# One-tile input loads, and work that changes engine, in a one-core hybrid mLSTM and DeltaNet block

## The chip, the cores and the metric

The kernel runs on one core of one Trainium2 chip. The metric is device time in microseconds (us); lower is better. A core has a matrix engine (TensorE, PE in the profile), an elementwise engine (VectorE, DVE), an activation engine (ScalarE, ACT), a general engine (GpSimd, POOL) and a synchronising engine (SyncE, SP) that here only issues transfers. Each engine runs its instructions in the order in which they stand in its own queue. Transfers are issued from SyncE, ScalarE or GpSimd and stand in the issuing engine's order until they are issued.

## The reference

One decoder layer over 512 tokens of width 2048, in float32:

```python
u = _rmsnorm(h, norm_w)
proj = jnp.matmul(u, w_in)                    # 24624 output columns
# mLSTM branch: 8 heads, q and k of 128, v of 256, exponential input gate, running-max stabiliser
# DeltaNet branch: 16 heads of 128; causal conv of width 4 and SiLU on q, k, v;
#   q and k divided by their L2 norms; chunks of 64:
lhs = strict_lower(beta * (k @ k.T) * decay) + eye
w_val, w_k = solve(lhs, [v * beta, k * beta * exp(gam)])
# recurrence over chunks: u = w_val - w_k S ; o = q_dec S + (qk*decay) u ; S = g S + k_end^T u
y_a = h_a @ w_out[:2048];  y_b = h_b @ w_out[2048:]
out = rmsnorm(h + sigmoid(gate_a) * y_a + sigmoid(gate_b) * y_b) * final_norm_w
```

## The kernel before

**Arithmetic.** Each float32 operand of a large product is split into two parts, hi and lo (`split_hi` is a cast on ScalarE, line 144; `split_lo` a subtraction on VectorE, line 147), and TensorE runs three products: hi with uh, hi with ul, lo with uh (lines 258 to 260 in `proj_cm`, 583 to 585 in the seven-product stage, 1423 to 1425 in the output stage).

**Stages.** First x is loaded, turned on TensorE (`make_u`, line 313), weighted by the norm weights and split into uh and ul, while the first block of input-projection columns is being multiplied (`proj_cm` with `before=first_block`). The token factor 1/rms comes later, from `square_x`. Then come the remaining first projections and a long stage of products (`seven_stage`) to about 1130 us, eight DeltaNet units of two heads each (`dn_unit`), in whose products the mLSTM heads are interleaved, and the output projection with the final norm.

**Order of the work.** TensorE's order is the order of the code. On the other engines a planner sorts by its own simulated times and priorities; `urgent` raises the priority, and `behind("A")` puts an instruction after the newest cast on ScalarE ("V": the newest lo split). Transfers on SyncE are sorted by the same planner.

**Steps.** Six large products make one call of `tick()`, called a step below. Everything of the mixers is written as generators started with `start(gen, wait)`; `yield n` means n steps later. A DeltaNet unit has 48 steps: 16 each for k, v and q.

**The start (lines 264 to 346).** x is held in four tiles, one for each 128 tokens. `load_x(a, b)` issues one transfer for each of them, alternately from SyncE and ScalarE, in five calls with column ranges that widen; weight tiles (`load_raw`, SyncE, 256 KB) stand between the first ones. `load_norms` loads the norm weights on GpSimd's queue and turns them on TensorE (line 109) before x. `make_u(kt)` turns one 128-column slice with four transposes; uh is written by ScalarE (line 314), ul by VectorE (line 315). Slices 0 to 3 stand ahead of the first product: two from the loop over `UA`, two from `before`.

**A DeltaNet unit.** After k's projection `conv_silu` and `silu_end` make k, and `turn` with `travel` make a token-major copy `ke`: a transpose in 32 x 32 blocks on VectorE, four transfers to DRAM and one back, all on SyncE. `dn_front_k` forms k k^T times the decay into `aq` and reads the key norms off its diagonal (line 926, VectorE), from which come `nk` and `cs` = beta over the squared norm. `aq` is scaled by cs (lines 941 to 944, ScalarE), its diagonal 32 x 32 blocks go through DRAM into `ls`, and 31 substitution passes on VectorE (lines 970 and 972, two to a step) invert them into `xi`; `xi` goes through DRAM into `tt`, and VectorE transposes that into `tn` (line 988). Counting steps from the end of k's projection, cs stands at 10, the scaling at 13 and 14, the first pass at 24, the transfers of xi at 39 and tn at 55. `dn_back` joins the blocks into the inverse of 128 x 128 in products p1 to p4, with evictions between them (s1, tb, ta, s3). For the second head of a unit the norm factor has not been multiplied in yet on one block; the eviction of p3 (line 1057) does it on 64 partitions on VectorE while ScalarE negates the other 64 (line 1056). The products of line 1063 read the first half. `dn_back` also multiplies v by the norms `nk` (line 1035). `dn_chain` then runs the recurrence.

Of the kernel before, what the change touches and what calls it, by code (L numbers as in the profile page):

```python
# [58 lines left out]
def hybrid_body(  # L59
# [119 lines left out]
    def split_next():  # L179
        raw, nk, n = raws[len(parts)]  # L180
        with tc.high_priority(offset=2 * PRIO if len(parts) > SAHEAD else 0):
            hi = wp.tile([P, nk, n], F32R, tag="wh", name="wh", bufs=NSPL)
            lo = wp.tile([P, nk, n], F32R, tag="wl", name="wl", bufs=NSPL)
            with ExitStack() as first:
                if len(parts) == 1:
                    first.enter_context(tc.issue_after(done["V"]))
                    first.enter_context(tc.issue_after(done["A"]))
                split_hi(hi, raw)
                split_lo(lo, raw, hi)
        parts.append((hi, lo))  # L190
# [56 lines left out]
    def proj_cm(col0, before=None):  # L247
        ps = [psj.tile([P, S], F32, tag="pj", name="pj") for _ in range(2)]
        for kt0 in range(0, KT, KP):
            hi, lo = next_w("i", col0, kt0)  # L250
            if before is not None:
                for k in range(KP):
                    before(kt0 + k)
            for j in range(2):
                for k in range(KP):
                    kt = kt0 + k
                    wsl = slice(j * P, (j + 1) * P)
                    T.matmul(ps[j], hi[:, k, wsl], uh[:, kt, :], start=(kt == 0), stop=False)  # L258
                    T.matmul(ps[j], hi[:, k, wsl], ul[:, kt, :], start=False, stop=False)  # L259
                    T.matmul(ps[j], lo[:, k, wsl], uh[:, kt, :], start=False, stop=(kt == KT - 1))  # L260
                tick()
        return ps
# [4 lines left out]
    load_norms(p0, psw)  # L267
    xts = [p0.tile([P, D], F32, tag=f"x{c}", name=f"xt{c}") for c in range(NC)]

    def load_x(a, b):  # L270
        for c in range(NC):
            (nc.scalar if c % 2 else nc.sync).dma_start(xts[c][:, a:b], x[c * P:(c + 1) * P, a:b])

    load_x(0, NB)
    load_raw()
    load_x(NB, 2 * NB)
    load_raw()
    for a in range(2 * NB, D, NO):
        load_x(a, a + NO)
    wg = p0.tile([P, KT, 48], F32, tag="wg", name="wg")  # L280
# [12 lines left out]
    def square_x(c, i):  # L293
        xt, at = xts[c][:, i * HD:(i + 1) * HD], ss[:, c, i:i + 1]
        jk = p0.tile([P, HD], F32, tag="jk", name="jk", bufs=2)
        with tc.issue_after(done["V" if i else "A"]):
            if i:
                V.scalar_tensor_tensor(out=jk, in0=xt, scalar=1.0, in1=xt, op0=ALU.mult, op1=ALU.mult, accum_out=at)
            else:
                A.activation(jk, xt, AF.Square, accum_out=at)  # L300
# [8 lines left out]
    def make_u(kt):  # L309
        pool, tg = ((psw, "wk"), (pso, "o"))[kt % 2]  # L310
        pt = pool.tile([P, S], F32, tag=tg, name="put")
        for c in range(NC):
            T.transpose(pt[:, c * P:(c + 1) * P], xts[c][:, kt * P:(kt + 1) * P], ident)
        done["A"] = A.activation(uh[:, kt, :], pt, AF.Copy, scale=normc[:, kt:kt + 1]).ins
        done["V"] = V.scalar_tensor_tensor(out=ul[:, kt, :], in0=pt, scalar=normc[:, kt:kt + 1],
                                           in1=uh[:, kt, :].bitcast(F32), op0=ALU.mult, op1=ALU.subtract).ins

    UA = 2
    for kt in range(UA):
        make_u(kt)  # L320
# [548 lines left out]
    def travel(o, dst, out, apart):  # L869
# [13 lines left out]
        yield 4  # L883
# [4 lines left out]
    def dn_front_k(hs, kq, u):  # L888
# [26 lines left out]
        for j in range(2):  # L915
# [6 lines left out]
            with urgent():  # L922
                V.tensor_tensor(out=aq[:, :, 0, :], in0=pk, in1=u["dm"][j][0], op=ALU.mult)
                jk = wkb.tile([P, P], F32, tag="jd", name="jd", bufs=1)
                for c in range(NC):
                    V.scalar_tensor_tensor(out=jk, in0=aq[:, c, 0, :], scalar=1.0, in1=ident, op0=ALU.mult,
                                           op1=ALU.mult, accum_out=nk[:, j, c:c + 1])
            yield 1
        V.tensor_scalar(out=nk, in0=nk, scalar1=EPS, scalar2=None, op0=ALU.add)
# [5 lines left out]
        yield 3  # L935
# [29 lines left out]
        for i in range(BS - 1):  # L965
# [7 lines left out]
            if i % 2:  # L973
                yield 1
# [11 lines left out]
        yield 16  # L986
# [25 lines left out]
    def dn_back(hs, kq, u):  # L1012
# [19 lines left out]
        for j in range(2):  # L1032
            vn = u["vs"][j]
            with behind("V"):
                V.tensor_tensor(out=vn, in0=vn, in1=bc(u["nk"][:, j, :], P), op=ALU.mult)
# [7 lines left out]
        with urgent(2):  # L1043
            V.tensor_copy(ta[32:64, :, 0:32], p2[32:64, 1])
        for q in range(2):
# [9 lines left out]
        with urgent():  # L1055
            A.mul(s3[64:128], p3[64:128], -1.0)
            V.tensor_tensor(out=s3[0:64], in0=p3[0:64], in1=u["cs"][0:64, 1, :].unsqueeze(2).to_broadcast([64, NC, 64]),
                            op=ALU.mult)
# [5 lines left out]
        with urgent():  # L1064
            V.tensor_copy(tb[0:64, 0:NC, 64:128], p4[0:64])
            A.mul(tb[0:64, NC:2 * NC, 64:128], p4[64:128], -1.0)
# [68 lines left out]
    def dn_unit(p):  # L1135
# [7 lines left out]
        for j in range(2):  # L1143
# [3 lines left out]
            start(silu_end(kq[j][:, 0, :], (kq[j][:, 0, :], ke)), 4 + 3 * j, front)  # L1147
# [653 lines left out]
```

## Time and profile before

| what | us |
|---|---|
| median of three runs | 2156.34 |
| lowest and highest | 2155.92, 2158.04 |
| the profiled execution's own time | 2156.07 |
| its span, first to last instruction | 2154.3 |
| TensorE busy | 2119.7 (98%) |
| VectorE busy | 1735.1 (81%) |
| ScalarE busy | 1043.4 (48%) |
| GpSimd busy | 453.5 (21%) |

All views are of one profiled execution on the chip; times start at its first instruction. The page gives busy time for each engine. The view of waits gives, for an engine, the time it sat idle before an instruction and what ended that. The time line lists instructions in order, with start, duration, engine, line, tile names and shapes, and in brackets the idle time before them. In the view of one line three numbers are the shortest, the median and the longest duration in nanoseconds. A view of stretches gives the busy time of each engine between two moments. In names, `put` is turned x, `pj` a projection in PSUM, `wr`, `wh` and `wl` a weight tile as loaded and its two parts.

### The profile page before, as it was taken

How to read it: one execution, taken by the hardware profiler on the slowest of the kernel's cores; microseconds unless marked ns; L12 is line 12 of the kernel's file. 1: busy time of each engine (PE TensorE's matmuls, PEld its weight loads, DVE VectorE, ACT ScalarE, POOL GpSimd, SP SyncE). 2: the span in 40 equal slices, each digit the busy share in tenths (PEclk: the TensorE clock that was granted, in tenths of full speed). 3: DMA queues.
4: the chain of work that ended last, by engine and by line, in shares of the span. 5: the costliest groups of instructions: out<-in, count | busy, mean ns of one | idle time of the engine just before them, and what ended most of it. 6: DMA issues, size and time to landing. Idle time of an engine off the chain costs nothing.

```text
span 2154.3 us, 32062 instructions
## 1 busy us (share of the span) xinstructions
PE 2119.7 (98%) x10545; PEld 1754.5 (81%) x10545; DVE 1735.1 (81%) x3035; ACT 1043.4 (48%) x2022; POOL 453.5 (21%) x690
## 2 busy tenths in 40 slices
PE   8999999999999999999999999999999999999998
PEld 6888888888888888888888888888888878787786
DVE  4888788788888777777858898988888888569887
ACT  4444455445544554454445536546455454345345
POOL 0000000000004000000013434326243263243211
PEclk9999999999999999999999999999999999999999
DMA  5456666667667766776766677668687677678895
GB/s 170 147 171 208 209 202 206 202 216 226 210 220 244 244 211 209 233 232 195 250 213 175 169 183 187 174 168 201 178 206 174 161 185 207 192 227 281 243 298 226
DMA packets 448961, 444.48 MB, mean 206 GB/s; under 512 B 197333, under 2 KB 305082, under 8 KB 448666
## 3 DMA queue, kind: packets, MB, share of 16 engines
q1 hardware_dynamic: 377882, 335.12, 53.5%
q0 software_dynamic: 24864, 73.17, 10.8%
q10 hardware_dynamic: 46048, 34.16, 4.9%
q8 instruction: 82, 1.34, 0.3%
q14 instruction: 85, 0.70, 0.1%
HBM read 348.92 MB, written 97.59 MB: 207 GB/s over the span
## 4 chain that ended last, share of the span: by engine, by line
PE 69%; issue 12%; DVE 8%; DMA 5%; ACT 3%; POOL 1%; SPq 1%; ACTq 0%; DVEq 0%; POOLq 0%
PE ps L584 14%; PE ps L585 14%; PE ps L583 14%; PE pj L258 6%; PE pj L260 6%; PE pj L259 6%; DVE wl L147 2%; PE py L1423 1%; PE py L1424 1%; PE py L1425 1%; ACT wh L144 1%; DVE kq L843 1%; DVE xi L972 1%; DVE tmp L970 1%; ACT njk L860 1%
## 5 line engine op out<-in xcount | busy, mean ns | idle before, releaser
L144 ACT CAST wh<-wr 128x512 fp32r<-128x512 f32 (+1 forms) x522 | 374.2, 717 | 416.4 <-PE pj L259 201.9
L147 DVE TENSOR_TENSOR wl<-wr,wh 128x512 fp32r<-128x512 f32 (+1 forms) x522 | 436.6, 837 | 162.1 <-ACT wh L144 158.2
L258 PE MATMUL pj<-uh,wh 128*128 128x512 f32 x896 | 375.9, 420 | 4.4 <-ACT wh L144 3.9
L260 PE MATMUL pj<-uh,wl 128*128 128x512 f32 x896 | 351.9, 393 | 0.0
L259 PE MATMUL pj<-ul,wh 128*128 128x512 f32 x896 | 350.0, 391 | 0.0
L584 PE MATMUL ps<-wl,uh 128*128 128x512 f32 x752 | 292.7, 389 | 1.1 <-DVE wl L147 1.1
L583 PE MATMUL ps<-wh,uh 128*128 128x512 f32 x752 | 292.6, 389 | 0.8 <-DVE X L637 0.8
L585 PE MATMUL ps<-wh,ul 128*128 128x512 f32 x752 | 292.6, 389 | 0.0
L144 ACT CAST wh<-t 128x1024 fp32r<-128x1024 f32 x120 | 126.4, 1053 | 290.8 <-PE ps L585 186.2
L538 POOL DMA_DIRECT2D t_d<-ts x104 | 56.7, 545 | 922.2 <-DVE ts L525 844.6
L584 PE MATMUL ps<-wl,suh 128*128 128x512 f32 x624 | 242.9, 389 | 0.5 <-DVE wl L147 0.5
L583 PE MATMUL ps<-wh,suh 128*128 128x512 f32 x624 | 242.8, 389 | 0.0
L585 PE MATMUL ps<-wh,sul 128*128 128x512 f32 x624 | 242.7, 389 | 0.0
L144 ACT CAST wh<-ts 128x512 fp32r<-128x512 f32 x240 | 148.1, 617 | 187.3 <-DVE ts L543 158.8
L147 DVE TENSOR_TENSOR wl<-t,wh 128x1024 fp32r<-128x1024 f32 x120 | 146.8, 1223 | 82.3 <-ACT wh L144 81.9
L260 PEld LDWEIGHTS pj<-uh,wl 128*128 128x128 f32 x896 | 168.4, 188 | 37.6 <-DVE wl L147 0.5
L258 PEld LDWEIGHTS pj<-uh,wh 128*128 128x128 f32 x896 | 169.2, 189 | 35.7 <-ACT wh L144 4.3
L259 PEld LDWEIGHTS pj<-ul,wh 128*128 128x128 f32 x896 | 169.5, 189 | 28.5
L147 DVE TENSOR_TENSOR wl<-ts,wh 128x512 fp32r<-128x512 f32 x240 | 164.3, 685 | 32.7 <-ACT wh L144 31.2
L584 PEld LDWEIGHTS ps<-wl,uh 128*128 128x128 f32 x752 | 141.2, 188 | 30.7 <-DVE wl L147 1.5
L583 PEld LDWEIGHTS ps<-wh,uh 128*128 128x128 f32 x752 | 141.2, 188 | 30.6 <-DVE X L637 1.2
L585 PEld LDWEIGHTS ps<-wh,ul 128*128 128x128 f32 x752 | 141.2, 188 | 29.2
(355 smaller groups left out, 3833.8 us busy)
## 6 DMA issues: line engine op xcount, KB each, us to landing
wr<-in_w_in_dram SPq DMA_DIRECT2D x744, 256.0 KB, 3.6
wr<-in_w_out_dram SPq DMA_DIRECT2D x138, 256.0 KB, 4.9
t_d<-ts POOLq DMA_DIRECT2D x104, 256.0 KB, 3.6
wr<-t_d SPq DMA_DIRECT2D x104, 256.0 KB, 3.8
tg_d<-X ACTq DMA_DIRECT2D x16, 256.0 KB, 4.3
tg_d<-to ACTq DMA_DIRECT2D x16, 256.0 KB, 4.1
v<-v_d SPq DMA_DIRECT2D x8, 512.0 KB, 6.1
mg<-g_d SPq DMA_DIRECT2D x16, 256.0 KB, 3.6
```

The source lines that it names most:

```text
L144: newest["A"] = A.copy(hi, src).ins
L147: newest["V"] = V.tensor_tensor(out=lo, in0=src, in1=hi.bitcast(F32), op=ALU.subtract).ins
L258: T.matmul(ps[j], hi[:, k, wsl], uh[:, kt, :], start=(kt == 0), stop=False)
L259: T.matmul(ps[j], hi[:, k, wsl], ul[:, kt, :], start=False, stop=False)
L260: T.matmul(ps[j], lo[:, k, wsl], uh[:, kt, :], start=False, stop=(kt == KT - 1))
L538: queue.dma_start(t2_d[b % 2, i], ts[:, 0, :])
L583: T.matmul(ps[t], ah, hi, start=(g == "A" and i == 0), stop=False, skip_group_check=True)
L584: T.matmul(ps[t], ah, lo, start=False, stop=False, skip_group_check=True)
L585: T.matmul(ps[t], al, hi, start=False, stop=(i == KH - 1), skip_group_check=True)
L843: V.scalar_tensor_tensor(out=dst, in0=yp[:, j:j + S], scalar=convc[:, 48 * j + ct:48 * j + ct + 1], in1=dst, op0=ALU.mult, op1=ALU.add)
L860: A.activation(jk, pk[:, c, :], AF.Square, accum_out=dst[:, c:c + 1])
L970: V.tensor_tensor(out=tv, in0=ls[:, i, i + 1:BS].unsqueeze(1).to_broadcast([P, m, n]), in1=xi[:, 0:m, i].unsqueeze(2).to_broadcast([P, m, ...
```

## The change

In the start, x becomes one tile of all four token blocks, and each range of columns (a slab) is one transfer on SyncE. A weight tile is loaded between all slabs, so that five are ahead instead of two. A Square of two ones is put first on ScalarE. The first slab is issued ahead of the norm weights. The first weight tile is split right behind slice 0's uh and ul, and slices 2 and 3 are turned between the two column halves of the first products, instead of before both.

In a unit, the key norms are taken by ScalarE from the turned copy `ke` (sum of squares, `token_norms`) instead of by VectorE from the diagonal. The v factors go to ScalarE in eight multiplications. The eviction of p3 becomes one negation of all 128 partitions on ScalarE; the factor cs is multiplied into `ta` on GpSimd before, and p4's second half is then copied without a sign. Several waits are set anew: the read back of a turned tile comes a step sooner, k's second copy starts a step sooner, cs comes at step 15, the scaling at 17 and 18, the first pass at 28, and the wait behind the passes is 12 instead of 16. In the last unit alone four passes go to a step.

```diff
@@ split_next
-                if len(parts) == 1:
+                if len(parts) < 2:
                     first.enter_context(tc.issue_after(done["V"]))
                     first.enter_context(tc.issue_after(done["A"]))
@@ proj_cm
-            if before is not None:
-                for k in range(KP):
-                    before(kt0 + k)
             for j in range(2):
+                if before is not None and j == (kt0 == 0):
+                    for k in range(KP):
+                        before(kt0 + k)
                 for k in range(KP):
@@ the start
+    xt = p0.tile([P, NC, D], F32, tag="x", name="xt")
+    warm = p0.tile([P, 2], F32, tag="warm", name="warm")
+    A.activation(warm, ones2, AF.Square)
+
+    def load_x(a, b):
+        nc.sync.dma_start(xt[:, :, a:b], x[:, a:b].rearrange("(c p) d -> p c d", p=P))
+
+    load_x(0, NB)
     load_norms(p0, psw)
-    xts = [p0.tile([P, D], F32, tag=f"x{c}", name=f"xt{c}") for c in range(NC)]
-
-    def load_x(a, b):
-        for c in range(NC):
-            (nc.scalar if c % 2 else nc.sync).dma_start(xts[c][:, a:b], x[c * P:(c + 1) * P, a:b])
-
-    load_x(0, NB)
     load_raw()
     load_x(NB, 2 * NB)
     load_raw()
     for a in range(2 * NB, D, NO):
         load_x(a, a + NO)
+        load_raw()
...
     UA = 2
-    for kt in range(UA):
-        make_u(kt)
+    make_u(0)
+    split_next()
+    make_u(1)
@@ travel
-        yield 4
+        yield 3
         with urgent(2):
             nc.sync.dma_start(dst, d.rearrange("(n j) r a c -> (j r) n (a c)", n=NC))
@@ dn_front_k
                 V.tensor_tensor(out=aq[:, :, 0, :], in0=pk, in1=u["dm"][j][0], op=ALU.mult)
-                jk = wkb.tile([P, P], F32, tag="jd", name="jd", bufs=1)
-                for c in range(NC):
-                    V.scalar_tensor_tensor(out=jk, in0=aq[:, c, 0, :], scalar=1.0, in1=ident, op0=ALU.mult,
-                                           op1=ALU.mult, accum_out=nk[:, j, c:c + 1])
             yield 1
+        yield 2
+        for j in range(2):
+            with behind("A"):
+                token_norms(u["ke"][j], nk[:, j, :])
+            yield 2 - j
...
-        yield 3
+        yield 2
         for j in range(2):
             aq = u["aq"][j]
...
-            if i % 2:
+            if i % 4 == 3 or (i % 2 and hs[0] < 2 * UNITS[-1]):
                 yield 1
...
-        yield 16
+        yield 12
         with urgent(), behind("V"):
             V.transpose(tn.rearrange("p g m -> p (g m)"), tt.rearrange("p g t -> p (g t)"))
@@ dn_back
-            with behind("V"):
-                V.tensor_tensor(out=vn, in0=vn, in1=bc(u["nk"][:, j, :], P), op=ALU.mult)
+            with behind("A"):
+                for c in range(NC):
+                    A.mul(vn[:, c, :], vn[:, c, :], u["nk"][:, j, c:c + 1])
...
             V.tensor_copy(ta[32:64, :, 0:32], p2[32:64, 1])
+        G.tensor_tensor(out=ta[:, NC:], in0=ta[:, NC:], in1=u["cs"][0:64, 1, :].unsqueeze(2).to_broadcast([64, NC, 64]),
+                        op=ALU.mult)
...
         with urgent():
-            A.mul(s3[64:128], p3[64:128], -1.0)
-            V.tensor_tensor(out=s3[0:64], in0=p3[0:64], in1=u["cs"][0:64, 1, :].unsqueeze(2).to_broadcast([64, NC, 64]),
-                            op=ALU.mult)
+            A.mul(s3, p3, -1.0)
...
             V.tensor_copy(tb[0:64, 0:NC, 64:128], p4[0:64])
-            A.mul(tb[0:64, NC:2 * NC, 64:128], p4[64:128], -1.0)
+            A.copy(tb[0:64, NC:2 * NC, 64:128], p4[64:128])
@@ dn_unit
-            start(silu_end(kq[j][:, 0, :], (kq[j][:, 0, :], ke)), 4 + 3 * j, front)
+            start(silu_end(kq[j][:, 0, :], (kq[j][:, 0, :], ke)), 4 + 2 * j, front)
```

`square_x` and `make_u` read the one tile instead of four.

More of the change, by code (lines that the diff above doesn't have):

```diff
@@ L293, in square_x @@
     def square_x(c, i):
-        xt, at = xts[c][:, i * HD:(i + 1) * HD], ss[:, c, i:i + 1]
+        at = ss[:, c, i:i + 1]
+        xc = xt[:, c, i * HD:(i + 1) * HD]
         jk = p0.tile([P, HD], F32, tag="jk", name="jk", bufs=2)
@@ L297, in square_x @@
             if i:
-                V.scalar_tensor_tensor(out=jk, in0=xt, scalar=1.0, in1=xt, op0=ALU.mult, op1=ALU.mult, accum_out=at)
+                V.scalar_tensor_tensor(out=jk, in0=xc, scalar=1.0, in1=xc, op0=ALU.mult, op1=ALU.mult, accum_out=at)
             else:
-                A.activation(jk, xt, AF.Square, accum_out=at)
+                A.activation(jk, xc, AF.Square, accum_out=at)
     def token_factors():
@@ L312, in make_u @@
         for c in range(NC):
-            T.transpose(pt[:, c * P:(c + 1) * P], xts[c][:, kt * P:(kt + 1) * P], ident)
+            T.transpose(pt[:, c * P:(c + 1) * P], xt[:, c, kt * P:(kt + 1) * P], ident)
         done["A"] = A.activation(uh[:, kt, :], pt, AF.Copy, scale=normc[:, kt:kt + 1]).ins
```

## The prediction

> **What bounds the kernel now.** I read the stretches first, to see where TensorE is not busy (columns: stretch, length, then busy time of PE, PEld, DVE, ACT and POOL, the granted clock, the DMA share, GB/s):
>
> ```profile
> 0.00:54.00 54.00, 43.94 (x212) 34.63 (x213) 25.96 (x49) 24.59 (x42) 3.49 (x14) 1.00 0.58 171
> 54.00:1140.00 1086.00, 1085.53 (x4807) 898.55 (x4806) 875.62 (x1163) 514.70 (x739) 88.09 (x161) 1.00 0.66 212
> 1140.00:1835.00 695.00, 686.76 (x4077) 572.21 (x4076) 591.33 (x1459) 362.84 (x1003) 279.38 (x396) 1.00 0.73 182
> ```
>
> TensorE bounds it. The opening leaves 10.1 us idle, the next 1086 us only 0.5, the DeltaNet units (1140 to 1835) 8.2. So the change can take time out only at the start and in the units, and what it takes out at the start reaches the end unless a later wait gives it back. From 1100 us on, TensorE's longest waits are these (total, times, longest):
>
> ```profile
> PE p L1063 <- DVE s L1057: 5.3, 4, 1.7
> PE py L1424 <- DVE wl L147: 2.8, 1, 2.8
> PE pw L1093 <- DVE r L1088: 1.5, 2, 0.8
> ```
>
> **The start.** The time line of ScalarE, then that of TensorE:
>
> ```profile
> 0.74 9.86 ACTq L272 DMA_DIRECT2D xt<-in_x_dram  x10
> 10.69 1.28 ACT L314 ACT_TABLE_LOAD   x1 [10.69 <-DMA xt<-in_x_dram]
> 11.99 1.26 ACT L314 ACTIVATE uh<-put,normc 128x512 fp32r<-128x512 f32 x2
> 13.14 0.62 ACT L144 CAST wh<-wr 128x512 fp32r<-128x512 f32 x1
> ```
>
> ```profile
> 4.97 0.25 PE L109 MATMUL pprm<-ident,nrow 16*128 16x16 f32 x1 [4.97 <-DMA nrow<-in_norm_w_dram]
> 5.16 2.39 PE L313 MATMUL put<-ident,xt 128*128 128x128 f32 x10
> 8.38 1.54 PE L313 MATMUL put<-ident,xt 128*128 128x128 f32 x6 [0.84 <-DMA xt<-in_x_dram]
> 13.81 0.79 PE L258 MATMUL pj<-uh,wh 128*128 128x512 f32 x1 [3.88 <-ACT wh L144]
> ...
> 16.64 0.60 PE L258 MATMUL pj<-uh,wh 128*128 128x512 f32 x1
> 17.07 0.42 PE L259 MATMUL pj<-ul,wh 128*128 128x512 f32 x1
> 17.33 0.39 PE L260 MATMUL pj<-uh,wl 128*128 128x512 f32 x1
> 17.56 0.39 PE L258 MATMUL pj<-uh,wh 128*128 128x512 f32 x1
> ...
> 18.26 0.93 PE L313 MATMUL put<-ident,xt 128*128 128x128 f32 x7
> ```
>
> ScalarE issues ten x transfers until 10.60, then loads its table, then makes uh and the first weight cast; only then, at 13.81, can the first product run, though sixteen transposes were ready at 9.92. The change takes the x transfers off ScalarE and has the table loaded by a two-column Square at the beginning, beside the wait for x.
>
> The new order is worked out from these rows. The transposes still begin at 5.16: the first TensorE instruction waits for the norm weights, which nothing moves, and x's first 256 columns had landed by then although they shared the queues. Four transposes at 0.24 (2.39/10) end at 6.1, one uh (1.26/2 = 0.63) at 6.75, the cast (0.62) at 7.4. Six products at the early spacing of 0.43 (16.64 to 17.07) then run to 10.0. The next eight transposes, now behind them, take 1.06 (0.93/7 each) to 1.9; the other six products take 1.4 (17.33 to 17.56 is 0.23) to 2.6. The following transposes so begin at 12.4 to 14.5 in place of 18.26: a gain of 3.8 to 5.9. I take 13.1, **-5.2 us**, with the clock rising in the middle.
>
> The spacing falls from 0.43 to 0.23 some 3.3 us after the first product, though transposes had run from 5.16 to 9.92. The Trainium skill, "TensorE: Matmul & The Clock Gate", section "Part 4: PE-mode transpose", says that transposes do not count as activity that releases the clock, which speaks against putting eight of them between the first products; the trace fits it, but its 3.9 us pause would explain the same. By that rule the slow end of my bounds, -3.8, would hold.
>
> What has to follow does so with cover. One SyncE queue now carries five slabs of x (4 MB) with the weight tiles between them. Queued behind are the fifth weight tile, which must wait for the first split to free its buffer (due about 8.4, before the queue gets there), the gate weights and the small parameters. The slabs for the next products are the second and third of five, and those were already the order of the old queues. If the cover were gone, a slab or the gate weights would be late by up to 2 us: that is inside the bounds.
>
> **The units.** Rows of the line view (min/median/max ns):
>
> ```profile
> L926 DVE SCALAR_TENSOR_TENSOR jd<-aq,ident x64: 248/292/1032, 1146.5 to 1756.7; 128x128 f32<-128x128 f32 x64
> L926 DVE DVE_READ_ACCUMULATOR jd<-aq,ident x64: 74/81/84, 1146.7 to 1756.9; 128x1 f32 x64
> L860 ACT ACTIVATE njk<-qn x64: 292/310/313, 1211.3 to 1833.7; 128x128 f32<-128x128 f32 x64
> L860 ACT ACTIVATION_READ_ACCUMULATOR njk<-qn x64: 185/187/190, 1211.5 to 1833.9; 128x1 f32 x64
> L1035 DVE TENSOR_TENSOR vt<-vt,nk x16: 678/684/882, 1224.7 to 1849.1; 128x512 f32<-128x512 f32 x16
> L944 ACT ACTIVATE aq<-aq,cs x32: 384/387/402, 1152.3 to 1758.9; 128x128 f32<-128x128 f32 x32
> ```
>
> Each of the eight units takes from VectorE 8 x (0.292 + 0.081) = 3.0 us of key norms, 2 x 0.684 = 1.4 of value factors and one 0.4 eviction: 4.8. It gives ScalarE 8 x (0.310 + 0.187) = 4.0 and 8 x 0.387 = 3.1: 7.1. The eviction's sign half was on ScalarE already; it now takes all 128 partitions at the same free length. Where that eviction stands (ScalarE's half, VectorE's half, and the stretch around, in the fourth unit):
>
> ```profile
> 1498.16 0.38 ACT L1056 ACTIVATE s<-p 64x256 f32<-64x256 f32 x1
> 1500.94 0.41 DVE L1057 TENSOR_TENSOR s<-p,cs 64x256 f32<-64x256 f32 x1
> 1486.00:1498.00 12.00, 12.00 (x144) 9.74 (x144) 8.62 (x29) 8.31 (x25) 8.12 (x12) 1.00 0.94 246
> ```
>
> ScalarE's half is 2.8 us ahead of VectorE's, which is the one that TensorE waits for, 1.3 us on average in four units. Moved whole to ScalarE, the 5.3 us of waits go, unless ScalarE becomes later by more than 2.8 - 1.3 = 1.5 us. It was busy 8.3 of those 12 us; 7.1 come and the 3.2 of the key scaling (4 x 0.387 and eight shorter ones) move four steps later, so 12.2 of 12: just full. I take **-4.5**, between -5.3 and 0. The multiplication by cs goes to GpSimd, with two waits of three steps (eleven microseconds at the step worked out below) before TensorE reads it; the stretch above has GpSimd busy 8.1 of 12 us, so it is covered: 0, and the wait itself, up to 1.5 a unit, if the queue there is that late. Less work on VectorE should end some of the 1.5 us at L1088: **-0.5** (0 to -1.5). A crowded ScalarE may hold the split of the weights or a state copy: **+0.5** (0 to +5).
>
> The key norms now come from the turned tile, so they wait on ScalarE for its round trip through DRAM, with the next weight casts behind them, and VectorE and TensorE behind those. The turned tile is written two steps after its SiLU, at 6 and 8, and its norms stand at 12 and 14: six steps, 10.9 us, against a trip of about 8.7 (both below). So 2 us are spare. The steps that the code counts go from 10 to 15 for cs and from 24 to 28 for the first step of the inverse, and the wait behind the inverse is cut from 16 to 12, so that its transpose tn stays at step 55. Its cover shrinks by four steps. Rows of VectorE and of TensorE:
>
> ```profile
> 1214.21 0.16 DVE L972 TENSOR_TENSOR xi<-xi,tmp 128x8 f32<-128x8 f32 x1
> ...
> 1222.96 0.45 DVE L988 STREAM_TRANSPOSE tn<-tt 128x256 f32<-128x256 f32 x1 [2.70 <-DMA tt<-xd]
> 1224.04 0.44 PE L1026 MATMUL p<-tn,aq 32*32 32x32 f32 x16
> 1461.51 0.17 DVE L972 TENSOR_TENSOR xi<-xi,tmp 128x8 f32<-128x8 f32 x1
> ...
> 1483.20 0.44 DVE L988 STREAM_TRANSPOSE tn<-tt 128x256 f32<-128x256 f32 x1
> 1838.18 0.45 DVE L988 STREAM_TRANSPOSE tn<-tt 128x256 f32<-128x256 f32 x1 [6.65 <-DMA tt<-xd]
> ```
>
> Three units from 1222.96 to 1483.20 give 86.7 us each, 1.81 a step (48 steps): four steps are 7.2 us. In the fourth unit the last step of the inverse precedes tn by 21.7 us and a trip takes about 8.7 (1214.21 to 1222.96), so 13.0 are spare and 7.2 cost nothing; I take the other middle units alike. The **first unit** has nothing spare: VectorE already waits there and TensorE needs tn 0.6 us after it is made. VectorE's work on the inverse's tile in the first 8.5 us (stretch, length, busy):
>
> ```profile
> 1170.00:1178.50 8.50, 3.73 (x16) 0.00 (x0) 1.00 0.85 194
> ```
>
> If the rest of VectorE's work fills the time around it, the inverse ends these 3.7 us later, else the whole 7.2; less 0.6, that is 3.1 to 6.6, or nothing if the relieved engine catches up. I take the work row, **+3.2**. The **last unit** has opposite edits: a start 7.2 later, but four inverse steps to a count instead of two. VectorE's 6.65 us wait for tt stands just before the 2.8 us that TensorE waits for wl. I take 0, between -2.8 (that wait goes) and +6 (the whole delay, TensorE needing tn about then). The read back of each turned tile comes one step sooner; its writes may then hold SyncE 1.8 us longer, but the weight tiles behind it are four deep: 0.
>
> Sum against the profiled execution's own 2156.07: -5.2 - 4.5 - 0.5 + 0.5 + 3.2 = -6.5, **2149.6 us**. The median shown is 0.3 above that execution, which changes nothing.
>
> **Rivals.** *All of it holds:* the inverse hides in both edge units. 2156.1 - 5.2 - 5.3 - 0.5 - 2.8 = 2142.3. For it: VectorE loses 4.8 us a unit. Against: the first unit's 2.70 us wait and the later start. *The wait changes its name:* the eviction is as late on the filled ScalarE, or GpSimd's product is. 2156.1 - 5.2 + 3.2 = 2154.1. For it: 12.2 of 12 us; against: the eviction is put first among what is ready. *ScalarE becomes the bound, the slower side:* it stands in order, and one unit's four microseconds of norms or the value factors in front of an urgent eviction make it late by as much. It decides from 1.5 us of lateness; with 4.0 each of eight units pays 2.5: 2156.1 - 5.2 - 5.3 + 3.2 + 8 x 2.5 = 2168.8. Against: ScalarE idles half of the units' stretch, 332 of 695 us. *The slabs do not part:* if one tile makes the first transposes wait for x's last slab, that is the landing of an issue at 10.6 with the longest trip of x's transfers,
>
> ```profile
> DMA to landing us min/median/max: 2.8/4.8/6.3
> ```
>
> so 16.9, and with 2.2 for transposes, uh and cast the first product comes at 19.1 instead of 13.8. But the eight later transposes leave their place before it, 1.9 at most: 2156.1 + 5.3 - 1.9 - 4.5 + 3.2 = 2158.2. Against: today's tiles take late columns while early ones are read, the transposes at 5.16.
>
> **Chances.** Forecast 0.48; all holds 0.22; changed name 0.15; ScalarE bound 0.07; slabs 0.03; mixtures 0.05. The range 2141 to 2157 holds the first three and the bounds of the edge units. A measurement of this kernel tells about 0.2%, 4.3 us, from no change. Faster by more: most of the forecast and all of the first rival, 0.68. Within: the rest of the forecast and the changed name, 0.21. Slower: 0.11.
>
> **What would show it.** The first product near 7.5 us and the second group of transposes near 10; no wait of L258 for the cast. No PE wait on the eviction s in units four to seven. In the first unit VectorE waiting more than 2.7 us for tt, and TensorE some 3 us at L1026. ScalarE's busy time in the units up by about 57 us, VectorE's down by 38. Wrong would be: waits of TensorE on ScalarE or GpSimd in every unit, a first transpose later than 6 us, or an opening that gains and a middle that idles again.

## The result, and the profile after

The changed kernel takes 2170.66 us in the median of four runs (2168.52 to 2172.88), beside 2157.1 for the kernel before: ratio 1.0063, 95% interval 1.0046 to 1.0081. It is 13.6 us slower, where the forecast was 6.5 faster (2149.6, range 2141 to 2157). The profiled execution took 2172.88, its span is 2170.8 (before 2156.07 and 2154.3).

The same stretches of the changed kernel, with the columns of the prediction:

```profile
0.00:54.00 54.00, 46.29 (x219) 35.45 (x219) 27.71 (x52) 25.79 (x46) 3.51 (x14) 0.97 0.57 175
54.00:1140.00 1086.00, 1086.00 (x4810) 899.36 (x4809) 876.74 (x1163) 515.04 (x741) 87.66 (x161) 1.00 0.66 212
1140.00:1835.00 695.00, 672.39 (x3991) 559.10 (x3990) 561.97 (x1272) 390.61 (x1158) 266.23 (x400) 0.99 0.70 176
```

The opening is fuller (46.29 busy us in place of 43.94) but not all of that is work: the clock is 0.97. In the units TensorE idles 22.6 us where it idled 8.2, though VectorE is busy 29 us less and ScalarE 28 more. (The stretches are fixed in time and the work runs up to 20 us later, so part of the last unit falls behind 1835: over the whole span VectorE is busy only 15 us less and ScalarE 38 more.) TensorE's waits of that stretch:

```profile
PE p L1031 <- DVE tn L993: 8.8, 1, 8.8
PE p L1047 <- ACT s L1036: 6.3, 12, 1.5
PE pj L258 <- DVE yp L838: 5.2, 7, 1.5
PE pw L1099 <- DVE r L1094: 1.8, 2, 1.5
```

The wait of the fourth products for `s` (5.3 before) is gone, as forecast. In its place stand three others: the inverse `tn` in the first unit, the second inverse step's `s1`, and `yp`, the copy that frees the PSUM tile in which a product was summed.

Where the time went is seen best by taking each large product's start in both traces. After minus before, us:

| place | offset |
|---|---|
| first product | -5.9 |
| 40 us into the opening | -1.5 |
| just before the first unit's inverse (1209) | +0.2 |
| just behind it (1238) | +11.2 |
| end of the sixth unit's second inverse step (1689) | +20.8 |
| output product that waited for `wl` before, ahead of it (1853.2) | +17.1 |
| behind it, before the last unit's inverse (1853.4) | +14.2 |
| behind that inverse (1863) | +18.5 |
| end of the span | +16.5 |

So the opening won and gave three quarters back. The first unit lost 11 at its inverse and had lost 2.4 before it, from 1160 us on, where TensorE waits 1.8 us for `yp`. The middle units lost 9.6 net until 1689 and regained 3.7 after it. The last unit lost 1.4: 3.0 won where a wait for `wl` is gone, 4.3 lost at its inverse. The profiled pair differs by 16.5 us in all, the medians by 13.6.

**The opening.** TensorE's time line:

```profile
5.50 1.97 PE L316 MATMUL put<-ident,xt 128*128 128x128 f32 x8
7.90 0.80 PE L258 MATMUL pj<-uh,wh 128*128 128x512 f32 x1 [0.43 <-ACT wh L144]
...
9.37 0.43 PE L258 MATMUL pj<-uh,wh 128*128 128x512 f32 x1
9.63 0.40 PE L259 MATMUL pj<-ul,wh 128*128 128x512 f32 x1
...
30.77 0.51 PE L258 MATMUL pj<-uh,wh 128*128 128x512 f32 x1 [0.93 <-ACT uh L317]
...
33.67 0.63 PE L260 MATMUL pj<-uh,wl 128*128 128x512 f32 x1
34.10 0.63 PE L258 MATMUL pj<-uh,wh 128*128 128x512 f32 x1
```

The first product is at 7.90 and products reach full spacing at 9.4. Near 31 us TensorE waits for `uh`, and from 33.3 the products stand 0.43 apart, half the clock, for 3.4 us. ScalarE, which makes `uh`, had itself waited for a weight tile, and SyncE's queue (second fence) shows what stood in front of that tile: two transfers of gate weights held the queue for 9.6 us, and eight small parameters followed; the tile was issued at 22.75.

```profile
28.84 1.30 ACT L144 CAST wh<-wr 128x512 fp32r<-128x512 f32 x2 [3.38 <-DMA wr<-in_w_in_dram]
```

```profile
7.58 2.80 SPq L333 DMA_DIRECT2D wg<-in_w_in_dram  x1
10.42 6.80 SPq L334 DMA_DIRECT2D wg<-in_w_in_dram  x1
```

**The first unit.** VectorE's time line, then TensorE's:

```profile
1222.40 0.18 DVE L977 TENSOR_TENSOR xi<-xi,tmp 128x8 f32<-128x8 f32 x1
...
1232.42 0.45 DVE L993 STREAM_TRANSPOSE tn<-tt 128x256 f32<-128x256 f32 x1 [7.68 <-DMA tt<-xd]
```

```profile
1233.02 1.06 PE L1031 MATMUL p<-tn,aq 32*32 32x32 f32 x32 [8.80 <-DVE tn L993]
...
1236.31 0.63 PE L259 MATMUL pj<-ul,wh 128*128 128x512 f32 x1
1236.74 0.63 PE L260 MATMUL pj<-uh,wl 128*128 128x512 f32 x1
```

The inverse's last pass is at 1222.40 in place of 1214.21, and its trip through DRAM takes 10.0 instead of 8.7. TensorE stands 8.8 us and runs at half clock behind the pause. The inverse itself was held up: VectorE's waits between 1165 and 1225 are

```profile
DVE wl L147 <- ACT wh L144: 3.5, 3, 1.7
DVE kw L870 <- DMA mkq<-qk_d: 2.2, 1, 2.2
DVE to L870 <- DMA td<-to: 1.1, 1, 1.1
```

and ScalarE, which makes `wh`, waited there 11.7 us for weight tiles (2.1 before):

```profile
ACT wh L144 <- DMA wr<-in_w_in_dram: 11.7, 4, 5.0
```

This wait comes with the norms: of the runs below, it is 10.7 in norms_only, and 2.1 in no_norms and in edge_old, whose first unit has the old norms.

**The middle units.** ScalarE in the fourth unit:

```profile
1503.41 1.86 ACT L1041 ACTIVATE vt<-vt,nk 128x128 f32<-128x128 f32 x6
...
1506.91 0.40 ACT L1041 ACTIVATE vt<-vt,nk 128x128 f32<-128x128 f32 x1
1507.34 0.78 ACT L1036 ACTIVATE s<-p 32x256 f32<-32x256 f32 x2
```

The first inverse products end at 1502.99; the eviction `s1` that the second ones need starts 4.4 us later, behind the eight multiplications of the value factors and some of the decay's exponentials, which stand between the rows shown.

### The profile page after: what moved, and what is told of

Its sections match the earlier page's. It is cut to its first block, busy times and chain, and to the rows that moved or that the text cites. A ratio compares the mean times of both kernels' runs of the same rounds, so it can differ in the third digit from the quotient of the medians.

```text
span 2170.8 us, 32130 instructions
## 1 busy us (share of the span) xinstructions
PE 2125.2 (98%) x10545; PEld 1758.1 (81%) x10545; DVE 1720.0 (79%) x2883; ACT 1081.9 (50%) x2215; POOL 443.3 (20%) x698
## 3 DMA queue, kind: packets, MB, share of 16 engines
q0 software_dynamic: 24864, 73.17, 10.9%
## 4 chain that ended last, share of the span: by engine, by line
PE 81%; DVE 7%; ACT 5%; DMA 3%; issue 2%; SPq 1%; ACTq 0%; POOLq 0%; POOL 0%; DVEq 0%
PE ps L588 17%; PE ps L587 17%; PE ps L589 17%; PE pj L258 6%; PE pj L259 6%; PE pj L260 6%; PE py L1429 2%; PE py L1431 2%; PE py L1430 2%; DVE tmp L975 1%; DVE wl L147 1%; DMA wr<-in_w_in_dram 1%; DVE xi L977 1%; ACT njk L864 1%; ACT wh L144 1%
## 5 line engine op out<-in xcount | busy, mean ns | idle before, releaser
L147 DVE TENSOR_TENSOR wl<-wr,wh 128x512 fp32r<-128x512 f32 (+1 forms) x522 | 430.2, 824 | 176.8 <-ACT wh L144 172.7
```

The lines of the kernel that those rows point to most:

```text
L147: newest["V"] = V.tensor_tensor(out=lo, in0=src, in1=hi.bitcast(F32), op=ALU.subtract).ins
```

## The experiments

All ratios are to the kernel before on the same chip, with 95% intervals; us are the ratio times 2156.

**The four parts, one at a time.** Each is the kernel before with some of the diff:

```diff
 open_only:  split_next, proj_cm, one xt tile in slabs, make_u order
 evict_only: + G.tensor_tensor(ta[:, NC:] * cs); A.mul(s3, p3, -1.0); A.copy(tb, p4)
 vn_only:    - V.tensor_tensor(vn * nk)   + A.mul(vn[:, c, :], ..., nk)  x8
 norms_only: + token_norms(ke) and its yields; yield 16 -> 12; travel yield 4 -> 3;
             second SiLU 4+3*j -> 4+2*j; last unit four passes a step
```

> The kernel before with the edits of the opening alone: x as one tile in slabs on SyncE's queue, the table load ahead, first turns between the first products; the units are as before. In the trace of the changed kernel the large products run 5.8 us ahead of the kernel before at 11 us and only 1.8 us ahead at 37 us. Theory C, the opening gives its gain back by itself (weight tiles late behind the gate weights on SyncE's queue, then a stretch at half clock): about -2 against the kernel before, some 2155, with the same 3.4 us idle of ScalarE near 25 us. Rival, the loss near 30 us is an accident of that one execution (the half clock may fall anywhere): -4 to -6, 2151 to 2153. My recorded forecast for this part was -5.2.

> The kernel before with the inverse's third eviction whole on ScalarE, the factor cs on GpSimd and the sign moved, nothing else. All theories that blame the norms, the value factors or the opening say that this part keeps what was forecast, -4 to -5.3: 2152 to 2153, and no wait of TensorE for s at the fourth products. Rival, GpSimd's multiplication or the filled ScalarE is as late as VectorE was: within 1 us of before.

> The kernel before with the value factors on ScalarE as eight multiplications a unit instead of two on VectorE, nothing else. Theory B, the order on ScalarE decides (value factors ahead of the second inverse eviction): TensorE waits for s1 at the second products as in the changed kernel, 6 us in all, +5 or more, 2162 or later. Theory A, the late inverse is the main loss: these waits come from the shift of everything else, and the value factors alone cost 0 to +2, 2157 to 2159.

> The kernel before with the key norms taken on ScalarE from the turned tile, with the later steps that follow (first step of the inverse four steps later, shorter wait behind it, earlier read back, last unit's four steps to a count), nothing else. Theory A, the late inverse in the first and last unit, and the half clock that follows its stalls, is the main loss: +14 to +18, 2171 to 2175, with TensorE waiting some 9 us for tn in the first unit and some 4 in the last. Theory B, ScalarE's order is the main loss: +5 to +9, 2162 to 2166, since the value factors are not there. My recorded forecast for this part was +3.

Measured:

| part | ratio | interval | us | forecast |
|---|---|---|---|---|
| opening | 0.9980 | 0.9970 to 0.9991 | -4.3 | -5.2 |
| eviction | 0.9977 | 0.9966 to 0.9987 | -5.0 | -4.5 |
| value factors | 1.0009 | 1.0000 to 1.0019 | +1.9 | about 0 |
| norms | 1.0047 | 1.0032 to 1.0062 | +10.1 | +3.2 |
| sum | | | +2.7 | -6.5 |
| changed kernel | 1.0063 | 1.0046 to 1.0081 | +13.6 | |

Theory A holds for the norms' place: with them alone TensorE has the tn waits of the changed kernel. Their size, +10.1, lies between the ranges of A and B. The value factors alone cost what A says. The opening's -4.3 is in the rival's range; its one profiled execution, the slowest of twelve, has the late tile and the half clock all the same. But the parts sum to 10.9 us less than the whole, more than the some 6 us that the intervals leave open: neither theory had that.

```profile
PE p L1027 <- DVE tn L989: 12.5, 2, 8.8
```

The eviction's run has the time that was forecast and another reason for it. TensorE's waits, then VectorE and GpSimd in the fourth unit:

```profile
PE pj L258 <- DVE yp L834: 5.6, 6, 1.3
```

```profile
1499.66 2.14 DVE L147 TENSOR_TENSOR wl<-wr,wh 128x512 fp32r<-128x512 f32 x1 [2.79 <-ACT wh L144]
1501.73 0.68 DVE L1267 TENSOR_TENSOR mg<-v,mg 128x512 f32<-128x512 f32 x1
1502.44 0.69 DVE L834 TENSOR_TENSOR yp<-pj,rsrow 128x512 f32<-128x512 f32 x1
```

```profile
1499.22 2.03 POOL L952 TENSOR_TENSOR dm<-dm,cs 128x512 f32<-128x512 f32 x2
```

In each of units four to seven the wait for `s` became a wait for `yp` 1.7 us later, of 1.0 to 1.3 us. VectorE is behind there, held by ScalarE's key scaling and by GpSimd's `dm`; the eviction had only been the first thing of VectorE that TensorE missed. So the forecast's -4.5 was met by luck. Against the kernel before the products are only 0.6 us ahead at 1781; the rest comes in the last unit and behind it (3.6 ahead at 1835), where the 2.8 us wait for `wl` is gone. Why it goes there was not tested.

**Which parts collide.** no_norms is the changed kernel without the norms' hunks, no_vn without the value factors', open_evict the opening and the eviction alone.

> The changed kernel with the key norms as before (on VectorE, from the diagonal of the product, with the old steps), but with the new opening, the value factors on ScalarE and the third eviction on ScalarE. The four parts taken one at a time moved the time by 0.998 (opening), 0.9977 (eviction), 1.0009 (value factors) and 1.0047 (norms), together -4.3 - 5.0 + 1.9 + 10.1 = +2.7 us, where all of them together made +13.6: 10.9 us are an interaction. Theory: the interaction needs the norms, because they make the inverse later and fill ScalarE so that the value factors stand ahead of the second inverse eviction. Then this kernel is the sum of its parts, -7.4, near 2148, and no wait of TensorE for s1. Rival, the value factors and the eviction collide by themselves: the waits for s1 are there and the time is 2155 or more.

> The changed kernel with the value factors back on VectorE, everything else as changed. Theory, the interaction is value factors with norms on ScalarE: the sum of the other parts holds, -4.3 - 5.0 + 10.1 = +0.8, near 2156, no wait for s1, the waits for tn of 9 and 4 us still there. Rival, the norms and the eviction (or the opening) interact without the value factors: 2162 to 2166.

> The kernel before with the new opening and the third eviction on ScalarE, the value factors and the norms on VectorE as before. By the sum of the two parts alone, -4.3 - 5.0: 2146. Theory, VectorE's backlog at that place: with the eviction alone TensorE's wait had only moved to the next thing it needs from VectorE, the convolution's input yp (5.6 us), and the value factors taken off VectorE shortened that to 2.4; so this kernel has the 5 us of waits for yp and is some 2 us above the kernel measured at 0.9961, near 2148.

no_norms: 0.9961 (0.9947 to 0.9975), -8.4 for a sum of -7.4. no_vn: 1.0032 (1.0021 to 1.0043), +6.9 for a sum of +0.8. open_evict: 0.9967 (0.9953 to 0.9980), -7.1 for -9.3. So the surplus needs the norms. TensorE's waits, no_norms first, then no_vn:

```profile
PE pj L258 <- DVE yp L838: 2.4, 3, 1.7
...
PE p L1046 <- ACT s L1035: 0.9, 5, 0.3
```

```profile
PE p L1031 <- DVE tn L993: 12.4, 2, 8.7
PE pj L258 <- DVE yp L838: 4.8, 7, 1.4
...
PE p L1046 <- ACT s L1036: 0.2, 1, 0.2
```

Two things add up to the surplus, the second of them argued only. The value factors cost little while ScalarE is not late (0.9 us of waits for `s1` in no_norms) and 6.3 us of waits once the norms are there too; from no_vn to the changed kernel is 6.7. And the norms' run has no wait for the fourth products' `s` either, so the eviction's gain is not there a second time: no_vn is 6 above its sum, at the lower end of the rival's range, and my expectation for it was wrong. No run has the norms and the opening without the eviction, which would show this. Taking the value factors off VectorE as well brings the waits for `yp` from 6.9 in open_evict to 2.4, as expected, but the two times (0.9967 and 0.9961) don't differ by more than their intervals.

**The value factors' place.**

```diff
         A.mul(s1[a1], p1[a1], -1.0)
-        for j in range(2): ... A.mul(vn[:, c, :], vn[:, c, :], u["nk"][:, j, c:c + 1])
 ...
             A.mul(s3, p3, -1.0)
+        for j in range(2): ... A.mul(vn[:, c, :], vn[:, c, :], u["nk"][:, j, c:c + 1])
```

> The changed kernel with one block moved: the eight multiplications of the value factors are asked of ScalarE behind the third eviction instead of ahead of the second product's (five steps later), so that they can't stand in front of s1. Theory, it is their place in ScalarE's order: the 6.3 us of waits for s1 and one half-clock stretch that follows them (1.7) go, 2160 to 2163. Rival, ScalarE is full whatever the order: the wait goes on to the third eviction or the state copies and the time stays at 2167 to 2171.

1.0216 (1.0200 to 1.0231): 47 us slower than before, 33 slower than the changed kernel. Both expectations fell. The waits for `s1` did go (0.4 left); but TensorE's waits are now

```profile
PE p L1031 <- DVE tn L993: 26.3, 3, 10.5
PE pr L1091 <- DVE st L1112: 11.9, 6, 2.2
```

and on ScalarE the block stands in the midst of the next unit's key norms:

```profile
1334.98 0.19 ACT L864 ACTIVATION_READ_ACCUMULATOR njk<-ke 128x1 f32 x1
1335.07 2.44 ACT L1064 ACTIVATE vt<-vt,nk 128x128 f32<-128x128 f32 x8
```

With the norms late the third unit's inverse ends at 1409.85, 8.0 us later than in the changed kernel, and it is late on SyncE too: eight writes of the next unit's keys now stand between its third and its fourth write (1412.67 to 1419.06). Its `tn` comes at 1426.8 (1412.6 in the changed kernel). The spare time before `tn` that the forecast had left to a middle unit, 13.0 less 7.2 us, was used up by a block of two and a half microseconds at the wrong place. The state copies that wait (`st`) are in the same units' chains; I did not separate the two.

**The edge units.** edge_old keeps the changed kernel but gives the first and last unit the old norms and waits; edge_back4 adds the old read back, edge_3j the old SiLU step in the second unit.

```diff
+        edge = hs[0] in (2 * UNITS[0], 2 * UNITS[-1])
+        if edge: V.scalar_tensor_tensor(jk, aq, ident, accum_out=nk)   else: token_norms(ke)
-        yield 12
+        yield 16 if edge else 12
 edge_back4: travel  - yield 3   + yield 4
 edge_3j:    silu_end  4 + (3 if p in (UNITS[0], UNITS[1], UNITS[-1]) else 2) * j
```

> The changed kernel with the key norms, their steps and the inverse's waits as before in the first and the last unit alone; the six units between keep the norms from the turned tile. The changed kernel is 13.6 above before. Theory A, the late inverse of the two edge units is what the norms cost (12.6 us of waits for tn, and some 8 us of half clock behind them, of which about 7 are lost): these go, 2148 to 2153, and only the 6 us of waits for s1 in the middle units are left. Rival, the middle units have no slack either: TensorE then waits for tn in the second unit or later, or the waits for s1 grow, and the time stays above 2158.

> The changed kernel with the old norms in the first and last unit, and with the read back of a turned tile four steps behind its writes again instead of three. In the run with the old norms in the edge units TensorE still waited 4.5 us for tn in the first unit: SyncE issued the inverse's read back (tt) 6.8 us behind its last write, 3.5 us in the kernel before, since a weight tile, eight writes of the second unit's turned keys (four in the kernel before), one read back of a turned tile and another weight tile stood in front of it. Theory, the earlier read back: with four steps tt stands ahead of it, the 4.5 us wait and the half clock of 6.83 behind it go, 2149 to 2152. Rival, the batch of eight writes is what counts: the wait stays at 3 to 4.5, 2156 to 2159.

> The changed kernel with the old norms in the first and last unit, and with the second SiLU of the second unit's keys three steps behind its first again instead of two, so that the writes of the two turned key tiles don't come together in front of the first unit's inverse on SyncE's queue. Theory, the batch of eight writes: four of them stand behind tt, the 4.5 us wait for tn and the half clock behind it go, 2149 to 2152. Rival, the earlier read back is what counts: the wait stays, 2156 to 2159.

edge_old: 1.0011 (1.0002 to 1.0020), 11 us below the changed kernel: the norms of two units of eight make half of the 22 us that lie between no_norms and it. That is the rival's time and not its mechanism, for TensorE still waits 4.5 for the first unit's `tn`. edge_back4: 1.0010 (1.0000 to 1.0020), the wait is 3.85. edge_3j: 0.9992 (0.9983 to 1.0001), that wait is gone. So in these runs it is the batch of writes, worth 4 us (each time is known to about 2). edge_3j is still some 2 us above its expected range and 7 above no_norms; it has 6.0 us of waits for `s1` in the middle units. SyncE's queue in edge_old (edge_back4 has the same order):

```profile
1212.79 2.62 SPq L996 DMA_DIRECT2D xd<-xi  x4
1215.51 0.55 SPq L176 DMA_DIRECT2D wr<-in_w_in_dram  x1
1216.15 4.33 SPq L886 DMA_DIRECT2D td<-ke  x8
1220.65 0.39 SPq L889 DMA_DIRECT2D ke<-td  x1
1221.08 0.52 SPq L176 DMA_DIRECT2D wr<-in_w_in_dram  x1
1221.64 0.47 SPq L997 DMA_DIRECT2D tt<-xd  x1
```

In edge_3j four of the second unit's key writes stand behind `tt`, which is issued 3 us after the inverse's last write instead of 6.2:

```profile
1211.86 2.62 SPq L996 DMA_DIRECT2D xd<-xi  x4
1214.57 0.55 SPq L176 DMA_DIRECT2D wr<-in_w_in_dram  x1
1215.22 2.11 SPq L886 DMA_DIRECT2D td<-ke  x4
1217.44 0.44 SPq L997 DMA_DIRECT2D tt<-xd  x1
```

**The opening's second half.**

```diff
 open_gq:   wg and parameters: nc.sync.dma_start -> nc.gpsimd.dma_start
 defer:     wg at kt == 1 -> 3, its split 6 -> 7, parameters 3 -> 9   (on no_norms)
 wg_behind: as defer, and each with behind("S"): nc.sync.dma_start(...)
```

> The kernel before with the new opening alone, and in it the gate weights (two transfers) and the small parameters (eight) go through GpSimd's queue instead of SyncE's, so that the weight tiles of the next products are not behind them. In the run with the opening alone ScalarE idled 3.4 us near 25 us for a weight tile that SyncE issued behind those ten transfers, TensorE then waited some 2 us and got half the clock for 3.41 us. Theory, that queue is the cause: no idle ScalarE there, no half clock near 33 us, the products stay 5.8 us ahead, and the time is 3 to 4 below the opening alone: 2147 to 2149. Rival, the weight tiles are late for want of bandwidth: the same waits, 2151.

> The changed kernel with the key norms as before (the kernel measured at 0.9961) and in its opening the two transfers of the gate weights issued two turns of the first block later, their split one turn later and the small parameters six turns later, all still on SyncE's queue. With the gate weights moved to GpSimd's queue the x slabs came late, so that run did not tell the order from the bandwidth. Theory C, the order on SyncE's queue gives the opening's gain back: the weight tile is in time, no half clock near 33 us, the products stay 5 to 6 us ahead at 40 us, and the time is 3 to 4 lower, 2142 to 2143. Rival, the 16 DMA engines are full until 20 us whatever the order: another tile is late, and the time stays at 2145 to 2148.

> The changed kernel with the key norms as before (measured at 0.9961), and on SyncE's queue the two transfers of the gate weights made to stand behind the sixth weight tile, the small parameters behind the ninth. In the run that issued them later in the code the trace shows the same order on the queue as before, so that run did not test it. Theory, the order on the queue gives the opening's gain back: ScalarE's wait for a weight tile near 25 us goes, the products stay 5 us or more ahead at 40 us, 2 to 3 less than the same kernel with the old order, 0.9947 to 0.9952. Rival, the DMA engines are full until 20 us whatever the order: the gate weights or a slab are then late, and nothing is gained, 0.9956 to 0.9966.

> The same kernel without the new order on the queue, measured beside it on the same chip: 0.9961 again, within 0.0015.

open_gq: 0.9985 (0.9976 to 0.9994). GpSimd issued the gate weights at 2.7 us, between the slabs, and TensorE waited 3.0 for x: neither expectation. defer: 0.9956 (0.9942 to 0.9970), but its queue has the old order, so it tells nothing of the order. wg_behind has the new order, and ScalarE's wait for the tile is gone: at 42 us the products are 4.6 us ahead of the kernel before, a little under the 5 expected and 1.6 more than in no_norms_again beside it. It measures 0.9949 (0.9935 to 0.9963) and no_norms_again 0.9952 (0.9939 to 0.9964): no difference. At 519 us this one wait takes the 1.5 back:

```profile
519.25 0.50 PE L590 MATMUL ps<-wl,suh 128*128 128x512 f32 x1 [1.46 <-DVE wl L147]
```

The kernel before waits 0.47 at the same product and no_norms_again not at all; both runs pass it 3.5 to 3.6 us ahead of the kernel before. This is no fixed limit: defer does not wait there and passes it 4.6 ahead. What holds the split `wl` at that point was not tested. Nor do the runs show that the order on the queue is the cause of the loss near 30 us. defer and edge_back4 have the old order, and in their profiled executions ScalarE waits 1.6 us for that tile, not 3.4; at 42 us their products are 4.0 and 4.3 ahead, where the nine other executions with the old order are 1.3 to 3.1 ahead. What decides when the tile lands stays open, and the new order shows no gain to the end.

The kernels without the norms beat both kernels: no_norms twice (0.9961 and 0.9952), wg_behind 0.9949, 2145.6 us beside 2156.8.

## Why the prediction was wrong

**The start, -5.2 (bounds -3.8 to -5.9).** The new order was right: 5.9 at the first product, and the second group of transposes begins at 10.10, as forecast; the slabs part. The term was too large: -4.3 alone, in the changed kernel -1.5 by 40 us. What failed is the sentence that "what has to follow does so with cover". I bounded the weight tiles' lateness by 2 us and kept it inside the -3.8; by 42 us TensorE had lost 4.4 of the 5.9, and between 1.2 and 3.7 in the runs with the same queue order and no half clock there. Why the tile lands sooner in some executions is open. In the Trainium skill, "TensorE: Matmul & The Clock Gate", section "Part 4: PE-mode transpose", transposes don't count as activity in the same way. The trace does not show their cost: full spacing came 1.5 us after the first product, behind 2 us of transposes, in place of 3.3. One execution does not prove that they count either, for the Trainium skill, "TensorE: Matmul & The Clock Gate", section "What's actually happening", has the window run free of the kernel. Two executions together do, on the grid of 3.41 us described at the end: in edge_old full clock followed a cell with 1.17 us of products and 1.82 of transposes, in norms_only a cell with 2.32 us of products and no transposes was followed by half clock. Here the measurement decides against the rule.

**The eviction, -4.5.** The waits for `s` went in all four units. The step that failed is taking "the 5.3 us of waits go" for 5.3 us won: I did not ask what TensorE misses next on VectorE. Alone, they were renamed to `yp`; with the norms moved, they would have gone without this edit. That is the rival "the wait changes its name", with VectorE and not ScalarE or GpSimd as the late engine. GpSimd's multiplication, costed at 0, cost nothing that a run showed.

**The first unit, +3.2 (3.1 to 6.6).** This is the step that made most of the miss. It cost 11.0 at the inverse, and 2.4 ahead of it that no term had. The mechanism, four steps later with nothing spare, was right; the size was not. I took the work row, 3.2, where the inverse ended 8.2 later, more than the four steps' 7.2, since VectorE idled inside it for transfers that SyncE brought late; the trip took 1.3 longer, and half clock followed the pause. **The read back, 0**, with "weight tiles four deep": the wrong thing was counted. In the first unit ScalarE waited 11.7 us for weight tiles all the same, and `tt` stands on that queue too. In edge_old it was the earlier SiLU (which I had read only as part of the norms' steps), not the earlier read back, that put eight writes ahead of `tt`: about 4 us, edge_old less edge_3j. In the changed kernel, whose inverse ends later, SyncE is done with these eight writes at 1222.85, 0.3 us behind the last pass; a read back and a weight tile follow, and the inverse's first write is issued at 1224.01. There they can explain part of the 1.3 us, not the rest.

**The last unit, 0 (-2.8 to +6).** The 2.8 wait went (-3.0), a wait of 3.84 for `tn` and half clock came (+4.3): +1.4, inside the bounds. Both of its opposite edits showed.

**ScalarE crowding, +0.5 (0 to +5), and VectorE's relief, -0.5.** The 12.2 of 12 us that I had worked out said that an in-order engine would be late somewhere; I spent it on the eviction alone. It was the value factors in front of `s1`, six units, 6.3 us; the rival "ScalarE becomes the bound" named this mechanism at 2.5 us in each of eight units and 0.07. Its 2168.8 is close to the measured 2170.7 by chance: the first unit made 13 of the profiled pair's 16.5. VectorE's relief did not show in the waits for `r`, 1.8 for 1.5. Over the whole span ScalarE's busy time rose from 1043.4 to 1081.9 and VectorE's fell from 1735.1 to 1720.0, less than the 57 and 38 I had named. On ScalarE, durations added one by one overlap: a key norm counted at 0.50 takes 0.30 to 0.42 from start to start, a value factor counted at 0.39 takes 0.31. VectorE's instructions became longer beside GpSimd (below).

## What to carry to other kernels

When a wait is to be removed, look at what the waiting engine needs next from the same late engine: if that engine is behind, the wait is renamed, not removed. When a step of a chain is moved earlier or later by counted steps, list for every queue which transfers come to stand in front of the chain's own; in edge_old four more small writes ahead of one read cost 4 us. Parts that each look harmless on a half idle in-order engine can collide: sum its load in the tightest stretch, not over the stage.

## What was not expected of the hardware

**VectorE is held by GpSimd.** In the kernel before, VectorE's and GpSimd's time lines in the fourth unit:

```profile
1498.78 1.53 DVE L1267 TENSOR_TENSOR mg<-v,mg 128x512 f32<-128x512 f32 x1
```

```profile
1497.17 2.58 POOL L952 TENSOR_TENSOR dm<-dm,cs 128x512 f32<-128x512 f32 x2
```

The same `mg` takes 0.68 at 1501.73 in evict_only, above, when GpSimd does not compute; `wl` took 2.14 there beside GpSimd in place of 0.69. Between 1140 and 1850 us of the kernel before, 49 VectorE instructions are over 0.3 us longer than the median of their line and shape, and all 49 overlap a computing instruction of GpSimd (of all 1472 there, 396 do); together they are 39.7 us longer. In the changed kernel 74 are longer, 70 of them with such an overlap, by 58.6 us in all: part of what was taken off VectorE came back this way. The Trainium skill, "SBUF — State Buffer", section "Who interferes with whom", says that a VectorE instruction with two SBUF inputs contends with a GpSimd instruction that reads SBUF, and that the later one is blocked until the first ends; these rows agree. It is part of what made VectorE late at the eviction.

**Half clock after short pauses.** Stretches at a granted clock of 0.5 lasted 3.41, 6.83, 10.24 and 13.65 us, one to four times the window of 3413 ns that the Trainium skill, "TensorE: Matmul & The Clock Gate", section "What's actually happening", gives: the trace agrees. The Trainium skill, "TensorE: Matmul & The Clock Gate", section "HAM oscillation — how this bites in real kernels", sets the danger at idle gaps above some 3.4 us. Here one such stretch, at 33.3, followed pauses of 0.93, 0.29 and 0.28 us; with the same opening and nearly the same pauses no_norms_again had none. So pauses below 1 us can be enough, and whether they are differs between executions.

The traces show what differs. All changes of the granted clock within one execution lie on a grid of 3.41 us. In the changed kernel one cell of it, 29.90 to 33.31, holds all three pauses, 1.54 us of idle time in all, and half clock follows; in no_norms_again a cell ends at 30.61, so that 0.55 falls into one and 0.98 into the next. Over the 17 profiled executions, up to 2135 us, each of the 30 drops to half clock follows a cell with at least 1.24 us idle, and no cell with more than 1.87 kept the full clock; of the 43 between, 11 were followed by a drop.
